# Low parts of the weights by a negative copy and an accumulating DMA, in one of two FFNs

## The chip, the cores and the metric

The kernel runs on one core of a Trainium2 chip. The metric is the time of one execution on the device in microseconds (us), median over runs. The engines are TensorE (PE, matmuls; its weight loads are listed as PEld), VectorE (DVE), ScalarE (ACT), GpSimd (POOL) and SyncE (SP, which here issues the DMAs).

## The reference

One inference step of a hybrid backbone over 128 context tokens and 512 latent tokens (640 columns), width 1024, two layers. Each layer has a token mixer (a recurrent mixer and two attentions) and then a gated FFN with a width-3 convolution on its gate half. The change concerns the FFN alone:

```python
def conv_ffn(h, lp):
    gate, val = jnp.split(h @ lp["w_up"], 2, axis=-1)
    gate = dwconv(gate, lp["ffn_conv_w"], lp["ffn_conv_b"], FFN_CONV_PAD_L)
    return (jax.nn.gelu(gate) * val) @ lp["w_down"]
...
    x = x + g2 * conv_ffn(modulate(x, lp["norm2_g"], sh2, sc2), lp)
```

Here w_up is 1024 x 5632 and w_down 2816 x 1024. All numbers are float32.

## The kernel before

Activations lie with features on the 128 partitions and tokens along the free dimension: eight chunks of 128 features by 640 columns, worked on in two halves of 320.

A float32 product is made of three matmuls in the shorter float32r type. Each operand is held as a high part (its value in float32r) and a low part (the rest, also float32r), and `mm3` (line 358) adds high x high, high x low and low x high into one bank. A weight tile of 128 x 1024 (eight blocks of 128 x 128) gives one chunk of 128 output features: per half 8 x 3 matmuls of 320 columns, so 48 matmuls for both halves (`gemm`, line 367).

`wload` (line 287) brings in such a tile. SP loads it into `wr` (line 291), ScalarE copies it into `wh`, which makes the high part (line 296), and VectorE subtracts `wh` from `wr` into `wl`, the low part (line 299). `wr`, `wh` and `wl` are rings of two buffers each (lines 206 to 208), so the weights of the chunk after next can be prepared once TensorE has finished the last chunk. In the stretch around the recurrent mixer the high part is made on VectorE instead (line 294).

The FFN (`ffn`, line 1355) starts with three gate chunks done together as the normed input comes in (`first`, line 380); the weights of two of them were brought in early by `first_weights` (line 337), those of the third by `wload` in line 1358. Then, in three groups of 8, 8 and 6 chunks, it takes turns: a gate chunk (from chunk 3 on: load in line 1373, evicted by ScalarE in lines 1334 to 1337, convolution and GELU in `ffn_gelu`, lines 1346 to 1352) and the value chunk to it (load in line 1380, multiplied onto the gate by VectorE in line 1385, and split into high and low part by lines 659 and 660). After each group `staggered` (line 1257) multiplies the group's 8 (or 6) chunks with the matching part of w_down: eight weight tiles, 1024 columns wide (768 in the last group), each result added to the residual by VectorE (line 1252). In the last group the sixth tile is split on VectorE by `wload_keys` (line 304).

The order of TensorE's work is set by `drive` (line 239), by a planned time. The other engines run their instructions in an order that a scheduler makes from dependences and priorities; `soon` (line 264) raises a priority, and line 292 raises that of the splitting a little. In each engine's queue an instruction that waits holds up all behind it. GpSimd has little to do in the FFN: three memsets of one column for each gate chunk (line 1330), which wait until the place of the pool is free.

Of the kernel before, what the change touches and what calls it, by code (L numbers as in the profile page):

```python
# [10 lines left out]
F32 = mybir.dt.float32  # L11
# [3 lines left out]
ALU = mybir.AluOpType  # L15
# [21 lines left out]
# columns of the per-feature vectors of one layer  # L37
# [6 lines left out]
# broadcast rows of one layer  # L44
# [8 lines left out]
class Slots:  # L53
    """Equal places of one tile, handed out in the order in which they came free; a place that
    another stream of work has used counts as `STRANGE` us younger."""
# [34 lines left out]
    def any_pair(self):  # L90
        """Two places wherever they are, as one operand of 2 x 512 columns."""
        a, b = sorted(self.get().at + self.get().at)
        return Slot(self.tile[:, a : b + 1 : b - a][:, :, :512], (a, b))
# [24 lines left out]
class Wide:  # L118
    """1024 columns over two places."""
# [21 lines left out]
class Stream:  # L141
    """Work whose next step may be issued `lag` us of TensorE's time after the last one, or
    once a mark has been set (and `lag` us after that)."""
# [28 lines left out]
class Net:  # L172
    NF = 22
    h_on_dve = False
    L_POOL, L_H = False, True
# [63 lines left out]
    def drive(self, streams):  # L239
        """TensorE takes its work in the order given here: the first stream that is ready."""  # L240
# [16 lines left out]
    def spawn(self, gen):  # L257
        """A stream that goes before all but the ones spawned earlier."""
        n = sum(s.spawned for s in self.streams)
        self.streams.insert(n, Stream("main", gen))  # L260
        self.streams[n].spawned = True
        self.streams[n].ready = self.t

    def soon(self, offset=None):
        """What frees a bank goes before other work of its engine."""
# [21 lines left out]
    def wload(self, src, place=None):  # L287
# [4 lines left out]
        with self.soon(self.WSOON) if self.WSOON else nullcontext():  # L292
# [4 lines left out]
            c = n // self.cut  # L297
            for o in range(0, n, c):
                self.sub_engine().tensor_tensor(  # L299
                    out=wl[:, o : o + c], in0=raw[:, o : o + c], in1=wh[:, o : o + c].bitcast(F32), op=ALU.subtract  # L300
# [3 lines left out]
    def wload_keys(self, src, low):  # L304
        """The same, the high parts behind the first weights in the place of the keys, the low ones in two of a pool."""
# [12 lines left out]
    def wload_wide(self, src, whole=False):  # L318
        """The same, into places of the two pools."""
# [17 lines left out]
    def first_weights(self, src, whole=False):  # L337
        """Weights that are there when h comes: the first in the place of the keys."""
# [19 lines left out]
    def mm3(self, out, a, b, first, last):  # L358
        """(ah + al) (bh + bl), without the product of the two low parts, which float32 can't hold"""
# [7 lines left out]
    def gemm(self, w, wofs, xs, lo, hi):  # L367
        """One output chunk over the columns lo..hi of the operands xs, into a bank."""
# [11 lines left out]
    def first(self, l, w, ws, evac):  # L380
        """The first products with h: one chunk of h after the other, as they come."""
# [15 lines left out]
    def setup(self):  # L397
# [9 lines left out]
        # silu(c) = 0.5 c (1 + tanh(c / 2))  # L407
# [9 lines left out]
    def setup_lru(self):  # L417
        nc = self.nc
        for l in range(DEPTH):
            # half biases of the recurrent gates  # L420
# [8 lines left out]
            # kk = -4 softplus(-lam); softplus(x) = max(x, 0) + log1p(e), e = exp(-|x|),  # L429
            # log1p(e) = 2 atanh(e / (2 + e))  # L430
# [20 lines left out]
    def mods(self, ahead=2):  # L451
        """The second norm's shift and scale (both conditions) of layer 0."""
# [30 lines left out]
        # chunk 4 j + b, condition i, sits in column b*128 + 32j + i  # L483
# [13 lines left out]
    def keep_cond(self):  # L497
        """silu(c) as rows, to be read by all partitions."""
# [17 lines left out]
    def mods_rows(self, l, v, pace, ahead=2):  # L516
        """One of the six modulation vectors of layer l: rows of w_mod times silu(c), summed along the row."""
# [36 lines left out]
    def square(self, x, m, half, eng=None):  # L554
        """Adds the squares of chunk m to the sums; the last chunk's stay apart."""
# [12 lines left out]
    def rstd(self, half, then=None):  # L568
        """1 / rms of every token of a half, in all partitions."""
# [28 lines left out]
        if half == 1:  # L598
            self.F.put(self.sqa, *self.sqb_)
            if then is not None:  # L600
                # the next table
# [3 lines left out]
    def modulated(self, l, w, k, half, t):  # L605
        """Chunk k of h = x * rstd * g (1 + scale) + shift, split in two parts, one half of the columns."""
# [17 lines left out]
    def norm_stream(self, l, w, half, name):  # L624
        """The norm of a half whose last chunk has just come."""
# [13 lines left out]
        else:  # L639
# [3 lines left out]
            while k < KC:  # L643
                # two chunks in one transfer where their places are in order
# [20 lines left out]
    def qkv(self, l, mx, hs):  # L665
# [8 lines left out]
        for g in range(3):  # L674
# [9 lines left out]
            for b in range(NB):  # L684
                bank = banks[b]
                if g < 2:
# [12 lines left out]
                    if b > 0:  # L699
                        # rotary of the latent q  # L700
# [25 lines left out]
        if mx == 0:  # L726
# [4 lines left out]
            # q: 1 / (8 rms), the score's scale within; k: 1 / rms  # L731
# [12 lines left out]
        # rotary of the latent k  # L744
# [13 lines left out]
    def keys(self, l, mx):  # L758
        """Both halves of every key side by side, transposed."""
# [36 lines left out]
    def attention(self, l, mx):  # L796
# [25 lines left out]
        def prepare(u):  # L822
            """What a unit needs before its scores: its q, split (turned later)."""
# [57 lines left out]
        def soften(x, lo, hi):  # L881
            """exp(score - max) of heads lo..hi, divided by its sum, from the banks."""
# [46 lines left out]
        def turn(x, lo, hi, ps):  # L929
            """The keys of a unit's probabilities into the partitions."""  # L930
# [81 lines left out]
    def lru(self, l, hs):  # L1012
        nc, io = self.nc, self.io
        self.oa, self.pend = [], deque()
        for n in range(KC):
# [34 lines left out]
            for half in range(2):  # L1050
                # 2 gelu(y) = y (1 + tanh(c0 (y + c1 y^3)))
# [25 lines left out]
    def lru_gates(self, l, oa, wg, n, xc, xch, xcl, gy):  # L1077
# [20 lines left out]
        for d in range(2):  # L1098
            # the input gate times x, twice over
# [3 lines left out]
        for d in range(2):  # L1103
            kk, nk = (self.kk[:, a, l, d * 8 + n : d * 8 + n + 1] for a in range(2))
            # log a = kk (1 + tanh); a; 1 - a^2 = tanh(-log a) (1 + a^2)
# [35 lines left out]
    def gate(self, l, row, hs, t):  # L1141
        """t = tanh(h Wg / 2) = 2 sigmoid(h Wg) - 1"""
# [577 lines left out]
```

## Time and profile before

| what | us |
|---|---|
| runs of the kernel before | 2416.93 and 2413.31, median 2415.12 |
| span of the profiled execution | 2408.8 |
| TensorE busy, of the span | 2377.8 |
| second layer's FFN with its entry and the final norm | from 1925 to 2409 of the span |

The page gives the profiled execution's time as its span, from the first to the last instruction; the time of a run holds start and end around it besides, and the median of the runs stands 6.3 us above the span. "Busy" is the time in which an engine had an instruction in work; matmuls are pipelined, so a busy TensorE need not be one at its peak. A wait is put down to the engine whose signal came last.

### The profile page before, as it was taken

The page shows a single profiled execution, that of the slowest core. Times are in us where ns is not written, and L with a number is a line of the kernel's source. Part 1 is how long each engine was busy: PE and PEld are TensorE (multiplying, and loading weights), DVE is VectorE, ACT ScalarE, POOL GpSimd, SP SyncE. Part 2 cuts the span into 40 slices and gives each one's busy share as a digit, 9 for nine tenths or more (in the row PEclk, how much of TensorE's full clock was granted, in tenths as well). Part 3 has the DMA queues.
Part 4 walks back from the last instruction along what each step waited for, and adds up shares of the span by engine and source line. Part 5 has one row for each costly group of instructions (what it writes and reads, how often), then busy time and mean ns, then how long its engine had stood idle before and what let it go on. Part 6 is the DMA issues. An engine that isn't in the chain of part 4 may idle for free.

```text
span 2408.8 us, 41835 instructions
## 1 busy us (share of the span) xinstructions
PE 2377.8 (99%) x16847; PEld 2301.7 (96%) x16847; DVE 1596.7 (66%) x3054; ACT 1006.4 (42%) x1958; POOL 17.9 (1%) x190
## 2 busy tenths in 40 slices
PE   8999999999999999999999999999999999999998
PEld 7899999998999999999999999999889999999998
DVE  6588878766766667686756688777568564344345
ACT  4237565733334322313343566565233343133232
POOL 0000000000000000000000000000000000000000
PEclk8999999999999999999999999999999999999999
DMA  8752222222452444354423222222227212222222
GB/s 284 237 191 73 83 79 76 88 75 79 146 183 75 138 140 151 130 167 148 147 87 131 89 92 70 83 85 87 69 68 230 80 62 71 79 76 73 79 68 76
DMA packets 124961, 267.73 MB, mean 111 GB/s; under 512 B 12240, under 2 KB 45536, under 8 KB 124768
## 3 DMA queue, kind: packets, MB, share of 16 engines
q1 hardware_dynamic: 124768, 265.07, 33.2%
q8 instruction: 132, 2.16, 0.4%
q14 instruction: 61, 0.50, 0.1%
HBM read 236.95 MB, written 28.07 MB: 110 GB/s over the span
## 4 chain that ended last, share of the span: by engine, by line
PE 86%; DVE 6%; ACT 3%; DMA 3%; issue 2%; SPq 0%; DVEq 0%; ACTq 0%
PE g L273 72%; PE s L273 4%; PE tb L273 4%; PE pv L273 3%; PE tb L277 3%; DVE wl L299 1%; DMA f<-in_wmodt 1%; DVE s L534 1%; ACT f L1091 1%; PE pv L277 1%; DMA f<-in_wmod 0%; DMA wr<-in_woc 0%; DVE f L1252 0%; ACT f L913 0%; DVE r L616 0%
## 5 line engine op out<-in xcount | busy, mean ns | idle before, releaser
L273 PE MATMUL g<-r,wh 128*128 128x320 f32 (+1 forms) x7920 | 1768.5, 312 | 2.9 <-ACT f L1148 0.9
L273 PEld LDWEIGHTS g<-r,wh 128*128 128x128 f32 x7920 | 1316.6, 188 | 20.5 <-issue 13.1
L273 PE MATMUL g<-r,wl 128*128 128x320 f32 (+1 forms) x3960 | 1222.3, 309 | 2.7 <-DVE wl L299 2.7
L273 PEld LDWEIGHTS g<-r,wl 128*128 128x128 f32 x3960 | 745.1, 188 | 3.8 <-DVE wl L299 3.8
L299 DVE TENSOR_TENSOR wl<-wr,wh 128x1024 fp32r<-128x1024 f32 (+2 forms) x291 | 334.8, 1151 | 224.5 <-ACT wh L296 219.6
L296 ACT CAST wh<-wr 128x1024 fp32r<-128x1024 f32 (+2 forms) x201 | 194.2, 966 | 494.9 <-PE g L273 424.4
L1252 DVE SCALAR_TENSOR_TENSOR f<-g,mod,f 128x128 f32<-128x128 f32 (+3 forms) x192 | 78.3, 435 | 138.7 <-PE g L273 138.6
L534 DVE SCALAR_TENSOR_TENSOR s<-f 128x1024 f32<-128x1024 f32 x128 | 157.2, 1228 | 15.8 <-DMA f<-in_wmodt 11.3
L891 DVE TENSOR_REDUCE sm<-s 128x1 f32<-128x640 f32 (+3 forms) x104 | 92.8, 892 | 89.1 <-PE s L273 88.6
L273 PE MATMUL g<-r 128*128 128x322 f32 (+3 forms) x632 | 124.2, 315 | 1.4 <-ACT f L1166 1.0
L273 PE MATMUL g<-wh,r 128*128 128x256 f32 x576 | 107.7, 282 | 0.0
L273 PEld LDWEIGHTS g<-r 128*128 128x128 f32 x632 | 100.4, 190 | 5.6 <-ACT f L1091 2.1
L1385 DVE TENSOR_TENSOR f<-f,g 128x320 f32<-128x320 f32 x88 | 42.5, 486 | 91.7 <-PE g L273 56.1
L659 ACT CAST r<-f 128x640 fp32r<-128x640 f32 (+2 forms) x98 | 70.3, 720 | 65.7 <-PE s L273 27.0
L273 PEld LDWEIGHTS g<-wh,r 128*128 128x128 f32 x576 | 90.4, 188 | 3.4 <-issue 3.4
L273 PE MATMUL s<-k,r 128*128 128x320 f32 (+3 forms) x448 | 92.3, 326 | 0.9 <-ACT k L787 0.9
L660 DVE TENSOR_TENSOR r<-f,r 128x640 fp32r<-128x640 f32 (+2 forms) x98 | 79.1, 812 | 15.8 <-ACT r L659 8.4
L913 ACT ACTIVATE f<-s,sm,rs 128x640 f32<-128x640 f32 (+1 forms) x80 | 63.5, 796 | 62.0 <-DVE sm L895 44.9
L1348 DVE SCALAR_TENSOR_TENSOR f<-f,vec 128x641 f32<-128x641 f32 x88 | 77.8, 887 | 13.6 <-ACT f L1346 8.4
L913 ACT ACTIVATE f<-s,sm 128x384 f32<-128x384 f32 (+2 forms) x80 | 45.6, 577 | 92.8 <-DVE sm L900 71.0
L273 PE MATMUL g<-wl,r 128*128 128x256 f32 x288 | 81.1, 282 | 0.0
L277 PE MATMUL tb<-ident,f 128*128 128x128 f32 x576 | 79.7, 272 | 0.0
(202 smaller groups left out, 2472.6 us busy)
## 6 DMA issues: line engine op xcount, KB each, us to landing
wr<-in_wup SPq DMA_DIRECT2D x84, 512.0 KB, 3.2
wr<-in_win SPq DMA_DIRECT2D x77, 512.0 KB, 3.3
f<-in_wmodt SPq DMA_DIRECT2D x64, 512.0 KB, 4.1
f<-in_wmod SPq DMA_DIRECT2D x64, 256.0 KB, 4.6
wr<-in_wdown SPq DMA_DIRECT2D x32, 512.0 KB, 3.4
wr<-in_wqkv SPq DMA_DIRECT2D x24, 512.0 KB, 3.6
g_kept<-f SPq DMA_DIRECT2D x32, 320.0 KB, 2.3
f<-g_kept SPq DMA_DIRECT2D x32, 320.0 KB, 3.7
```

The source lines that it names most:

```text
L273: self.nc.tensor.matmul(**kw)
L277: self.nc.tensor.transpose(out, in_, self.ident)
L296: nc.scalar.copy(wh[:, :n], raw[:, :n])
L299: self.sub_engine().tensor_tensor(out=wl[:, o : o + c], in0=raw[:, o : o + c], in1=wh[:, o : o + c].bitcast(F32), op=ALU.subtract)
L534: nc.vector.scalar_tensor_tensor(out=self.S, in0=w.ap, scalar=1.0, in1=self.cb[i].ap, op0=ALU.mult, op1=ALU.mult, accum_out=self.mod[:, l, ...
L659: nc.scalar.copy(xh[:, :n], t[:, :n])
L660: (eng or nc.vector).tensor_tensor(out=xl[:, :n], in0=t[:, :n], in1=xh[:, :n].bitcast(F32), op=ALU.subtract)
L891: nc.vector.tensor_reduce(out=m_[:, lo:hi], in_=src, axis=AX.XY if hi - lo == 1 else AX.X, op=ALU.max)
L913: nc.scalar.activation(out=p[:, :n].rearrange("p (a c) -> p a c", a=2) if hi - lo == 1 else p[:, o : o + n], in_=src if hi - lo == 1 else ...
L1252: self.nc.vector.scalar_tensor_tensor(out=dst[:, lo:hi], in0=b[:, lo - c0 : hi - c0], scalar=self.mod[:, l, gate + m, i : i + 1], in1=src[ ...
L1348: nc.vector.scalar_tensor_tensor(out=g[:, :n], in0=gp[:, k : k + n], scalar=fw(k), in1=g[:, :n], op0=ALU.mult, op1=ALU.add)
L1385: nc.vector.tensor_tensor(out=gp[:, lo:hi], in0=gp[:, lo:hi], in1=b, op=ALU.mult)
```

## The change

In the FFN of the second layer (`l == 1`) `wload` makes the low part in another way. ScalarE writes the negative of the raw weights into `wl`, which is rounded to float32r as the high part is; GpSimd then issues a DMA that adds the raw weights onto it, so that raw minus rounded is left. VectorE has no part in it. The switch is set at the start of `ffn`, so the weights loaded in line 1358 and all after it go this way: 42 tiles of w_up and 23 of w_down, 65 in all. The two early tiles of w_up and the tile of `wload_keys` stay on VectorE.

```diff
 class Net:
+    by_dma = False
...
     def wload(self, src, place=None):
...
-            c = n // self.cut
-            for o in range(0, n, c):
+            if self.by_dma:
+                nc.scalar.mul(wl[:, :n], raw[:, :n], -1.0)
+                nc.gpsimd.dma_start(out=wl[:, :n], in_=raw[:, :n], accum_op=ALU.add)
+            else:
                 self.sub_engine().tensor_tensor(
-                    out=wl[:, o : o + c], in0=raw[:, o : o + c], in1=wh[:, o : o + c].bitcast(F32), op=ALU.subtract
+                    out=wl[:, :n], in0=raw[:, :n], in1=wh[:, :n].bitcast(F32), op=ALU.subtract
                 )
...
     def ffn(self, l):
         nc, io = self.nc, self.io
+        self.by_dma = l == 1
```

The loop over pieces of a tile, which is taken out as well, made one piece everywhere (`cut` is 1). The rest of the diff is comments and doc strings. The changed kernel's lines are some three to four numbers higher.

The order of the engines' queues ahead of the second FFN is the same in both kernels. In it, ScalarE's queue is shown for one gate and one value chunk in the second group of eight. `wh_65` and `wl_67` are the buffers of the gate's weights, `wh_66` and `wl_68` those of the value's, `g` the banks. Before:

```order
L1334 COPY f<-g_74 128x128 [waits PE_49]
L1335 COPY f<-g_74 128x192
L296 CAST wh_65<-wr_63 128x1024 [waits DMAHW4_49,PE_49]
L1337 COPY f<-g_72 128x320 [waits PE_49]
L1346 ACTIVATE f<-f,vec 128x641 [waits Activation_49,Pool_49]
L1351 ACTIVATE f<-f 128x128 [waits DVE_49,Activation_49]
L1352 ACTIVATE f<-f 128x512
L296 CAST wh_66<-wr_64 128x1024 [waits DMAHW5_49,PE_49]
L659 CAST r<-f 128x640 [waits DVE_49,Activation_49]
```

Now:

```order
L1337 COPY f<-g_74 128x128 [waits PE_49]
L1338 COPY f<-g_74 128x192
L297 CAST wh_65<-wr_63 128x1024 [waits DMAHW4_49,PE_49]
L1340 COPY f<-g_72 128x320 [waits PE_49]
L299 ACTIVATE wl_67<-wr_63 128x1024 [waits DMASW0_49]
L1349 ACTIVATE f<-f,vec 128x641 [waits Activation_49,Pool_49]
L1354 ACTIVATE f<-f 128x128 [waits DVE_49,Activation_49]
L1355 ACTIVATE f<-f 128x512
L297 CAST wh_66<-wr_64 128x1024 [waits DMAHW5_49,PE_49]
L299 ACTIVATE wl_68<-wr_64 128x1024 [waits DMASW1_49,PE_49]
L662 CAST r<-f 128x640 [waits DVE_49,Activation_49]
```

The negative copies (L299) have come in: the gate's behind the eviction of the gate's second half, the value's right behind its cast and ahead of the split of the finished chunk.

GpSimd's queue in the first group, where the memsets of line 1330 (1333 now) prepare the next gate chunk. Before:

```order
L1330 MEMSET f 128x1 [waits DMAHW5_49,DMAHW2_49,DMAHW7_49,PE_49,Activation_49]
L1330 MEMSET f 128x1 [waits PE_49,Activation_49]
L1330 MEMSET f 128x1 [waits DMAHW2_49,Activation_49]
L1330 MEMSET f 128x1 [waits Activation_49]
L1330 MEMSET f 128x1 [waits DVE_49]
L1330 MEMSET f 128x1 [waits DMAHW7_49,DMAHW4_49,Activation_49]
```

Now, over one pair of chunks:

```order
L1333 MEMSET f 128x1 [waits Activation_49] x2
L300 DMA wl_68<-wr_64 128x1024 [waits DMAHW1_49,Activation_49]
L300 DMA wl_67<-wr_63 128x1024 [waits DMASW0_49,DMAHW2_49,PE_49,Activation_49]
L1333 MEMSET f 128x1 [waits DVE_49]
L1333 MEMSET f 128x1 [waits Activation_49,Pool_49] x2
L300 DMA wl_68<-wr_64 128x1024 [waits DMAHW3_49,DMASW1_49,Activation_49]
```

The accumulating DMAs (L300) stand between the memsets, the value's and the next gate's one behind the other. SP's queue keeps its order; its raw loads in this FFN wait for the accumulating DMA (and ScalarE) where they waited for VectorE.

## Rows read from the trace of the kernel before

**Rows 1.** The page's busy times: engine, us (share of span), instructions.

```profile
span 2408.8 us, 41835 instructions
...
PE 2377.8 (99%) x16847; PEld 2301.7 (96%) x16847; DVE 1596.7 (66%) x3054; ACT 1006.4 (42%) x1958; POOL 17.9 (1%) x190
```

**Rows 2.** Busy us of each engine in stretches of the second layer's FFN.

```profile
core 0: us, PE busy (x) PEld busy (x) DVE busy (x) ACT busy (x) POOL busy (x), PEclk, DMA share, GB/s
1925.00:1945.00 20.00, 19.61 (x136) 19.12 (x136) 18.47 (x50) 12.31 (x32) 0.20 (x2) 1.00 0.16 54
1945.00:2352.00 407.00, 407.00 (x2784) 406.96 (x2783) 167.64 (x220) 130.00 (x208) 5.31 (x54) 1.00 0.22 73
...
2395.00:2409.00 14.00, 4.66 (x37) 4.23 (x36) 9.32 (x23) 1.00 (x3) 0.00 (x0) 0.74 0.54 187
```

**Rows 3.** What PE waited for, 1925 to 2409 us: total, times, longest.

```profile
PE g L273 <- DVE f L1252: 0.4, 1, 0.4
PE g L273 <- DVE r L660: 0.2, 1, 0.2
```

**Rows 4.** ScalarE in order of time: start us, us, instruction [idle before <- releaser].

```profile
2114.42 1.05 ACT L296 CAST wh<-wr 128x1024 fp32r<-128x1024 f32 x1 [1.85 <-PE g L273]
2115.38 0.72 ACT L659 CAST r<-f 128x640 fp32r<-128x640 f32 x1
...
2121.44 1.05 ACT L296 CAST wh<-wr 128x1024 fp32r<-128x1024 f32 x1 [2.87 <-PE g L273]
2122.39 0.42 ACT L1337 COPY f<-g 128x320 f32<-128x320 f32 x1
2122.91 0.93 ACT L1346 ACTIVATE f<-f,vec 128x641 f32<-128x641 f32 x1
...
2128.46 1.05 ACT L296 CAST wh<-wr 128x1024 fp32r<-128x1024 f32 x1 [1.85 <-PE g L273]
```

**Rows 5.** Groups of instructions, 1941 to 2409 us: count | busy, mean ns | idle.

```profile
L299 DVE TENSOR_TENSOR wl<-wr,wh 128x1024 fp32r<-128x1024 f32 x56 | 68.6, 1225 | 107.7 <-ACT wh L296 107.7
L296 ACT CAST wh<-wr 128x1024 fp32r<-128x1024 f32 x56 | 58.8, 1050 | 189.4 <-PE g L273 181.1 <-issue 8.3
```

**Rows 6.** DMA issues of the whole span: count, KB each, median us to landing.

```profile
wr<-in_wup SPq DMA_DIRECT2D x84, 512.0 KB, 3.2
wr<-in_win SPq DMA_DIRECT2D x77, 512.0 KB, 3.3
...
wr<-in_wdown SPq DMA_DIRECT2D x14, 384.0 KB, 3.0
f<-in_x SPq DMA_DIRECT2D x16, 320.0 KB, 4.9
...
wr<-in_wob SPq DMA_DIRECT2D x16, 256.0 KB, 2.6
```

**Rows 7.** ScalarE in the last down-projection, in order of time.

```profile
2358.94 0.83 ACT L296 CAST wh<-wr 128x768 fp32r<-128x768 f32 x1 [0.71 <-PE g L273]
2359.68 0.41 ACT L561 ACTIVATE f<-f 128x256 f32<-128x256 f32 x1
...
2364.25 0.83 ACT L296 CAST wh<-wr 128x768 fp32r<-128x768 f32 x1 [0.75 <-PE g L273]
```

**Rows 8.** ScalarE at the entry of the FFN, in order of time.

```profile
1925.59 1.03 ACT L296 CAST wh<-wr 128x1024 fp32r<-128x1024 f32 x1
1926.52 0.47 ACT L564 ACTIVATE f<-f 128x320 f32<-128x320 f32 x1
```

**Rows 9.** PE at the entry of the FFN, in order of time.

```profile
1930.57 0.32 PE L273 MATMUL g<-r,wl 128*128 128x320 f32 x1
```

**Rows 10.** ScalarE behind the first products, in order of time.

```profile
1954.09 1.06 ACT L296 CAST wh<-wr 128x1024 fp32r<-128x1024 f32 x1
1955.04 0.93 ACT L1346 ACTIVATE f<-f,vec 128x641 f32<-128x641 f32 x1
...
1959.88 1.05 ACT L296 CAST wh<-wr 128x1024 fp32r<-128x1024 f32 x1 [0.23 <-PE g L273]
```

## The prediction

> **What bounds the kernel now.** The order of reading is: the page's busy times, the same by stretches, what TensorE waits for in the stretch that the change touches, the groups of instructions there, one period of that stretch in order of time, and last the transfers.
>
> The busy times say that TensorE (PE) works in 99% of the 2408.8 us and VectorE (DVE) in 66% [rows 1]. A share over the whole span hides the stages, so the stretches come next. In the second layer's FFN, from 1945 to 2352 us, PE is busy in 407.00 of 407.00 us at a granted clock of 1.00, the 2.4 GHz level, while VectorE has 167.64 us of work and ScalarE (ACT) 130.00 [rows 2]. So in this stretch an instruction taken from VectorE buys nothing by itself: VectorE idles for 239 us of it already. The list of PE's waits from the entry of the FFN to the end confirms it: apart from two waits of the final norm, PE waits 0.4 us at the entry and 0.2 us at the last group [rows 3]. The most that this change can win is about these 0.6 us.
>
> What matters is therefore how late a low part (wl) may come before PE has to wait for it. One set of weights feeds 48 matmuls. Two sets of buffers take turns, so a buffer that PE leaves must be filled again while PE works on the other set. A cast of the high part (line 296) starts when PE leaves a buffer; three of them in a row start at 2114.42, 2121.44 and 2128.46 [rows 4]: PE needs 7.02 us for a set, 0.146 us for a matmul. The first two matmuls of a set use the high part, so the low part is wanted 0.29 us after the set begins. From the start of the cast to that moment there are 7.02 + 0.29 = 7.31 us. Before, the cast (1.05 us) and VectorE's subtraction (1.23 us) [rows 5] filled about 2.3 of them, and 5 us were left over. That is the cover of this edit, and the question is whether it is thick enough.
>
> **What is removed.** 65 subtractions leave VectorE; 56 of them take 68.6 us in the FFN [rows 5]. By the paragraph above they hide beside PE, so I count them at nothing. Two stand in the entry, where VectorE has 18.47 us of work in 20 [rows 2] and PE's whole wait is 0.4 us [rows 3]; at most that goes, and I count nothing for it either.
>
> **What is added.** For each of the 65 weight sets ScalarE makes a negative copy, and GpSimd issues an accumulating DMA of 512 KB (384 KB for seven of them) from the raw weights onto it. No negative copy stands in the trace. The nearest row is the cast of the same shape, 1.05 us [rows 5]; it reads and writes the same bytes on the same engine, so the copy is taken as 1.05 us, between 0.95 (the distance at which the next instruction starts behind a cast, [rows 4]) and twice as much. ScalarE has room for 65 of these: 130 us of work in 407.
>
> Where it stands decides more. In the down-projections and for the value weights the copy follows its cast directly: the next instruction starts 0.96 us behind the cast (2115.38 against 2114.42) and the copy ends 0.96 + 1.05 = 2.01 us after the buffer came free. For the gate weights the eviction of a bank (line 1337, 0.42 us) stands between them, and the instruction behind that starts at 2122.91, 1.47 us after the cast; the copy ends at 2.52 us [rows 4]. So the DMA, from the end of the copy to the first matmul that reads its result, has 7.31 - 2.01 = 5.30 us in a down-projection and 7.31 - 2.52 = 4.79 us for a gate. Call the DMA's whole time L: the wait on GpSimd, the making of descriptors, the transfer and the signal. What L is above this room, PE waits.
>
> **How long is L?** Nothing in the trace accumulates, and GpSimd issues no transfer, so I bound it by the loads that SP issues [rows 6]. Issue to landing is 2.6 us for 256 KB, 3.0 for 384 and 3.2 to 3.3 for 512. The lower end is one plain pass of 512 KB, 3.3 us: it fits into both rooms. If the DMA only reads two streams instead of one, 256 KB more cost 0.7 us, so a second 512 KB cost 1.4 and L = 4.7; this fits as well, by a hair for the gates. If the sum waits for the destination to be read back, as two transfers one after the other, L = 2 x 3.3 = 6.6. The upper end is two passes at the slowest landing of the trace, 4.9 us (f<-in_x, at the kernel's busy start), so L = 9.8. I take 6.6: the destination must be read and written, the 16 DMA engines also carry the raw weights (a mean share of 0.22 here, [rows 2]), and GpSimd has to make the descriptors, for which the row of the plain load has no term.
>
> The Trainium skill speaks against this change, but not with one voice. "DMA: Bandwidth & Descriptors", Anatomy of one DMA, fits GpSimd's transfers by 2.0 us plus bytes over 436 GB/s: 3.2 us for a plain 512 KB, which the landings of SP's loads here agree with. "Collectives: The Full Stack", The bandwidth ceiling, says that an add in the DMA costs because it reads two sources; two reads by that fit give an estimate of 4.4 us, and the sum below would shrink to the first rival. The same DMA page, Bandwidth, has 6.15 us of engine time for 1 MB from GpSimd, before descriptors; by that estimate L lies above both rooms. No run here shows either.
>
> **The sum, at L = 6.6.**
> - Gate and value chunks: a pair of sets cannot turn faster than the gate's buffer: 2.52 + 6.6 + (7.02 - 0.29) = 15.85 us against 14.04, so each pair loses 6.6 - 4.79 = 1.81. There are 19 pairs (chunks 3 to 21): 34.4 us.
> - The two full down-projections, 16 sets: two sets lose 6.6 - 5.30 = 1.30, so 8 x 1.30 = 10.4.
> - Last down-projection, 768 columns: casts 5.31 us apart (2358.94, 2364.25), cast and copy 0.74 + 0.83, so the room is 5.31 + 0.3 - 1.57 = 4.0 us [rows 7]; the DMA has 384 KB, 2 x 3.0 = 6.0 [rows 6]. Two sets lose 2.0; its first two sets and the one on VectorE have more room, so two such pairs: 4.0.
> - Entry: the cast of the third up chunk starts at 1925.59, the next instruction at 1926.52 [rows 8], so its copy ends at 1927.57 and its low part lands at 1934.2. PE wanted it at 1930.57 [rows 9]: 3.6.
> - Behind the first products: cast at 1954.09, next at 1955.04 [rows 10], copy to 1956.09, landing 1962.7. PE leaves the set before it at 1959.88 and wants the low part at 1960.17: 2.5. One more turn of the same buffer, 1.3.
>
> Together 56 us. PE's clock is taken as kept: it is granted 1.00 where PE is busy 19.61 of 20 us and 0.74 where it is busy 4.66 of 14 [rows 2]; at 14.04 of 15.85 it stands near the first. Two queues could add to it and don't: the raw load on SP now waits for the DMA instead of the subtraction, but it needs 3.3 us and is wanted a set later; GpSimd's memsets stand behind the DMA, but each waits for the same gate chunk's GELU anyway. The profiled execution becomes 2408.8 + 56 = 2465 us; the median of the runs stands 6.3 us above that span (start and end around it), so 2415.1 + 56 = 2471 us, 2.3% slower. Each us of L is worth 32 us (19 + 8 + 5 single places), and 2%, about what a measurement of this kernel can tell from no change, is 48 us: the verdict turns at L = 6.35.
>
> **The rivals.**
> - *The transfer hides* (not slower). The add runs in the stream and L is at most about 5.5; at 4.7 only the entry (1927.57 + 4.7 - 1930.57 = 1.7 us) and the first value sets (0.6) lose, and the last group's split, which now stands behind a copy of 0.84 us on ScalarE, adds its delay to the 0.2 us of wait there: about 3 us, 2418. For it: the landing grows so little with size, and DMA engines are idle for 78% of the stretch. Against it: the room for the gates is 4.79 us, and GpSimd's own work comes off it. It decides below L = 5.5 (up to 21 us).
> - *The add is slow.* Read back, add and write come to 9.8 us: 56 + 3.2 x 32 = 158, 2573. For it: three times as many bytes pass the engines as for a load, in the same rows as the raw loads. Against it: nothing in the trace is that slow at 512 KB.
> - *VectorE was a bound after all.* Its 68.6 us would show as waits of PE on it; there are 0.6 us of these [rows 3]. At best 2414.5.
>
> **How the numbers follow.** Forecast, two passes with L between 5.5 and 8.5: 0.50, of which 0.12 lies below 6.35 and so within 2%; its own range is 2436 to 2532. The transfer hides: 0.33. The add is slow, beyond 8.5: 0.15. VectorE a bound: 0.02. Slower is 0.38 + 0.15 = 0.53, same 0.33 + 0.12 = 0.45, faster 0.02. The range goes from the hidden transfer, 2416, to 2575, the upper end of L.
>
> **What would show it.** Right: in the FFN of the second layer PE waits for the DMA of wl once in two sets; casts of line 296 follow each other about 7.9 us apart instead of 7.02; landing behind the copy is near 6.6 us; VectorE's work falls by some 70 us with no wait of PE gone. The step on the copy is wrong if it takes over 1.2 us; the step on the room if PE waits on ScalarE. The whole is wrong if landings stay under 4.8 us, or if PE's clock falls in the waits.

## The result, and the profile after

The changed kernel takes 2442.68 us (median of 2 runs, 2439.80 to 2445.56), against 2415.12 us before: a ratio of 1.0116, 95% interval 1.0082 to 1.0150. It is slower by 27.6 us, about half of the forecast 56 us; that is clear of no change, but less than 2%. The time lies in the range, which is wide: 2416 to 2575 goes from no change to 6.6% slower. It is neither the forecast (2471) nor the first rival (2418), but between them, and the reason for this is what the experiments are about.

Busy times of the page of the changed kernel, which answer to [rows 1], and the new queue of GpSimd (packets, MB, share of 16 engines' span):

```profile
span 2437.8 us, 41968 instructions
...
PE 2389.4 (98%) x16847; PEld 2309.3 (95%) x16847; DVE 1522.6 (62%) x2989; ACT 1064.8 (44%) x2023; POOL 74.0 (3%) x255
...
q0 software_dynamic: 9360, 33.17, 7.0%
```

VectorE lost 74 us of work and ScalarE gained 58, as the edit says. TensorE has the same 16847 matmuls, and yet 11.6 us more busy time. The span is 29.0 us longer, so TensorE's idle time grew by 17.4 us. That is two losses, and only one of them is waiting. They are found next in the stretches (engine busy us, count, then PE's granted clock, DMA share and GB/s):

```profile
1925.00:1935.00 10.00, 7.86 (x45) 7.37 (x44) 5.87 (x18) 4.77 (x11) 1.52 (x2) 0.83 0.75 156
1945.00:2090.00 145.00, 143.25 (x974) 142.20 (x973) 36.76 (x61) 63.06 (x91) 18.30 (x39) 1.00 0.56 135
2094.00:2104.00 10.00, 7.10 (x29) 7.10 (x30) 0.92 (x3) 0.00 (x0) 0.00 (x0) 0.66 0.39 96
2110.00:2120.00 10.00, 7.16 (x39) 6.90 (x38) 0.55 (x1) 2.49 (x4) 0.86 (x1) 0.83 0.83 183
2120.00:2270.00 150.00, 148.78 (x1015) 148.15 (x1014) 35.44 (x57) 66.25 (x96) 20.41 (x45) 1.00 0.60 146
2275.00:2285.00 10.00, 7.15 (x30) 7.15 (x31) 1.48 (x5) 0.00 (x0) 0.00 (x0) 0.66 0.39 98
2291.00:2301.00 10.00, 7.17 (x39) 6.90 (x38) 0.55 (x1) 2.49 (x4) 0.86 (x1) 0.83 0.84 186
2301.00:2380.00 79.00, 78.72 (x538) 78.37 (x537) 20.15 (x28) 39.44 (x62) 10.44 (x21) 1.00 0.57 139
```

Against [rows 2], where PE was busy in all of the stretch at a clock of 1.00, the long stretches (145, 150 and 79 us) lose 1.75, 1.22 and 0.28 us. Most of the loss sits in four places of about 10 us, two and two, and some of it at the entry (1925 to 1935). In each of the four PE stands for nearly 3 us, and the granted clock around it is below 1. What PE waited for, 1925 us to the end (total, times, longest), against [rows 3]:

```profile
PE g L274 <- DMA wl<-wr: 17.8, 12, 3.1
...
PE g L274 <- ACT f L1338: 0.5, 1, 0.5
PE g L274 <- ACT r L618: 0.5, 1, 0.5
```

Single rows of PE in order of time (start us, us, instruction, idle before and its releaser): the first products at the entry, the one behind them, and two of the four long waits, the first with its neighbours.

```profile
1927.04 0.53 PE L274 MATMUL g<-r,wh 128*128 128x320 f32 x2 [0.48 <-ACT r L618]
1929.23 0.63 PE L274 MATMUL g<-r,wl 128*128 128x320 f32 x1 [1.66 <-DMA wl<-wr]
...
1961.56 0.42 PE L274 MATMUL g<-r,wl 128*128 128x320 f32 x1 [0.56 <-DMA wl<-wr]
...
2096.90 0.63 PE L274 MATMUL g<-r,wl 128*128 128x320 f32 x1 [3.09 <-DMA wl<-wr]
...
2097.86 0.47 PE L274 MATMUL g<-r,wl 128*128 128x320 f32 x1
2098.13 0.73 PE L274 MATMUL g<-r,wh 128*128 128x320 f32 x2
...
2103.71 0.31 PE L274 MATMUL g<-r,wl 128*128 128x320 f32 x1
2103.86 0.46 PE L274 MATMUL g<-r,wh 128*128 128x320 f32 x2
...
2113.31 0.64 PE L274 MATMUL g<-r,wl 128*128 128x320 f32 x1 [2.84 <-DMA wl<-wr]
```

The other two long waits are of 2.89 us (to 2277.85) and 2.83 us (to 2294.24). Behind the first of them a matmul takes 0.27 us (2097.86 to 2098.13), at 2103.71 it takes 0.15 us again: the two levels of the clock, 1.2 and 2.4 GHz. A granted clock of 0.66 in 10 us is 6.8 us at the half level, 0.83 is 3.4 us; over the four places and the entry that makes 24 us, which cost about 12 us of matmul time. That is the growth of the busy time.

ScalarE and GpSimd in the steady part and at the first long wait (ScalarE's rows answer to [rows 4]):

```profile
2089.93 1.05 ACT L297 CAST wh<-wr 128x1024 fp32r<-128x1024 f32 x1 [5.02 <-PE g L274]
2090.89 1.05 ACT L299 ACTIVATE wl<-wr 128x1024 fp32r<-128x1024 f32 x1
...
2135.76 1.05 ACT L297 CAST wh<-wr 128x1024 fp32r<-128x1024 f32 x1 [2.88 <-PE g L274]
2136.71 0.42 ACT L1340 COPY f<-g 128x320 f32<-128x320 f32 x1
2137.03 1.06 ACT L299 ACTIVATE wl<-wr 128x1024 fp32r<-128x1024 f32 x1
...
2142.78 1.05 ACT L297 CAST wh<-wr 128x1024 fp32r<-128x1024 f32 x1 [1.11 <-PE g L274]
```

```profile
2092.23 0.86 POOL L300 DMA_DIRECT2D wl<-wr  x1 [6.17 <-ACT wl L299]
```

The steady casts still follow each other 7.02 us apart: the pairs of gate and value chunks lose almost nothing (three single waits in 19 pairs, of 0.80, 1.13 and 0.28 us). The groups and the DMA issues from 1941 and 1930 us on, against [rows 5, 6] (the DMA's last number is from the start of GpSimd's instruction to landing):

```profile
L299 ACT ACTIVATE wl<-wr 128x1024 fp32r<-128x1024 f32 x56 | 59.2, 1057 | 0.0
L300 POOL DMA_DIRECT2D wl<-wr x63 | 54.2, 860 | 354.7 <-ACT wl L299 344.9 <-ACT f L564 6.0 <-ACT f L567 3.8
```

```profile
wl<-wr POOLq DMA_DIRECT2D x56, 512.0 KB, 4.4
...
wl<-wr POOLq DMA_DIRECT2D x7, 384.0 KB, 3.8
```

The copy ends at 2091.94 us, GpSimd starts at 2092.23, 0.29 us later, and the landing takes 4.4 us: L, as the prediction defined it, is 4.7 us and not 6.6.

**Where the four long waits come from.** They stand at the eighth tile of each of the two full down-projections, and at the first gate tile behind it. The last two tiles of a down-projection are taken half by half (`staggered`, late = 2): first half of tile seven, first half of tile eight, second half of seven, second half of eight. So PE leaves tile six's buffer, works half a set (24 matmuls, 3.51 us), and wants tile eight in that same buffer. At the other end it leaves tile seven's buffer, has half a set of tile eight to do, and wants the next gate. The room is 3.51 + 0.29 = 3.80 us there, not 7.31. The path is cast and copy 2.01, GpSimd's start 0.29, landing 4.4: 6.7 us. The difference is 2.9 us, four times.

### The profile page after: what moved, and what is told of

Its sections match the earlier page's. It is cut to its first block, busy times and chain, and to the rows that moved or that the text cites. A ratio compares the mean times of both kernels' runs of the same rounds, so it can differ in the third digit from the quotient of the medians.

```text
span 2437.8 us, 41968 instructions
## 1 busy us (share of the span) xinstructions
PE 2389.4 (98%) x16847; PEld 2309.3 (95%) x16847; DVE 1522.6 (62%) x2989; ACT 1064.8 (44%) x2023; POOL 74.0 (3%) x255
## 3 DMA queue, kind: packets, MB, share of 16 engines
q0 software_dynamic: 9360, 33.17, 7.0%
## 4 chain that ended last, share of the span: by engine, by line
PE 79%; DVE 7%; DMA 5%; issue 4%; ACT 4%; SPq 0%; POOL 0%; DVEq 0%; ACTq 0%; POOLq 0%
PE g L274 65%; PE s L274 4%; PE tb L274 3%; PE pv L274 3%; PE tb L278 3%; DMA wl<-wr 2%; DMA f<-in_wmodt 2%; DVE s L537 1%; DVE wl L302 1%; ACT f L1094 1%; PE pv L278 1%; DMA wr<-in_woc 0%; ACT wh L297 0%; DMA f<-in_wmod 0%; ACT f L916 0%
## 5 line engine op out<-in xcount | busy, mean ns | idle before, releaser
L274 PE MATMUL g<-r,wl 128*128 128x320 f32 (+1 forms) x3960 | 1228.3, 310 | 21.9 <-DMA wl<-wr 17.8
L302 DVE TENSOR_TENSOR wl<-wr,wh 128x1024 fp32r<-128x1024 f32 (+2 forms) x226 | 257.4, 1139 | 109.2 <-ACT wh L297 97.9
L537 DVE SCALAR_TENSOR_TENSOR s<-f 128x1024 f32<-128x1024 f32 x128 | 157.4, 1230 | 16.8 <-DMA f<-in_wmodt 11.7
```

Source lines behind the costliest of these rows:

```text
L274: self.nc.tensor.matmul(**kw)
L302: self.sub_engine().tensor_tensor(out=wl[:, :n], in0=raw[:, :n], in1=wh[:, :n].bitcast(F32), op=ALU.subtract)
L537: nc.vector.scalar_tensor_tensor(out=self.S, in0=w.ap, scalar=1.0, in1=self.cb[i].ap, op0=ALU.mult, op1=ALU.mult, accum_out=self.mod[:, l, ...
```

## The experiments

My theory after this: (a) the loss of the stream is these four places, where the room is half a set; (b) each costs its wait and then the half clock behind it; (c) L is 4.7 us because the addition reads a second source. The rivals: the rest of the DMA traffic costs TensorE something everywhere; ScalarE's added copies do; the clock falls because of the DMA traffic and not because PE stood; the addition is free and GpSimd's transfers are that slow anyway.

Single spans scatter by some us before the FFN begins. So the table has, beside the medians, the stage's time in the profiled execution: from the start of PE's first wait at the FFN's entry to the start of its last waiting matmul in the final norm. For before and after these are the rows (a wait starts at the row's start less the idle time in brackets):

```profile
1930.20 0.54 PE L273 MATMUL g<-r,wh 128*128 128x320 f32 x2 [0.38 <-DVE f L1252]
...
2401.22 0.82 PE L273 MATMUL pv<-v,ones 128*128 128x128 f32 x4 [1.26 <-DVE v L588]
```

```profile
2430.13 0.68 PE L274 MATMUL pv<-v,ones 128*128 128x128 f32 x4 [1.26 <-DVE v L591]
```

Before: 2401.22 - 1929.82 = 471.4 us. After: 2430.13 - 1926.56 = 503.6. Runs e1 to e12 were taken in four rounds, each with the kernel before beside it (2410.8 to 2412.9 us), so it is the ratios that compare from row to row.

| run | edit | median us | ratio, 95% interval | stage, against before | PE's waits on wl |
|---|---|---|---|---|---|
| after | the change | 2442.7 | 1.0116, 1.0082 to 1.0150 | +32.2 | 17.8 in 12 |
| e1 | four short tiles back on VectorE | 2423.3 | 1.0045, 1.0029 to 1.0061 | +9.4 | 5.8 in 8 |
| e2 | these four alone by DMA | 2429.0 | 1.0071, 1.0058 to 1.0084 | +18.3 | 11.5 in 4 |
| e3 | third low buffer | 2421.8 | 1.0039, 1.0025 to 1.0053 | +11.1 | 1.7 in 1, and 3.9 in 1 on the third buffer |
| e4 | copies without DMA | 2415.3 | 1.0013, 1.0003 to 1.0024 | +2.3 | none |
| e5 | no half-by-half tiles | 2423.4 | 1.0045, 1.0030 to 1.0059 | +11.1 | 5.2 in 8 |
| e6 | the same order in the kernel before | 2412.3 | 1.0008, 0.9998 to 1.0017 | 0.0 | none |
| e7 | waits made on VectorE | 2438.8 | 1.0113, 1.0095 to 1.0131 | +27.0 | 18.0 in 4 (VectorE) |
| e8 | DMA without the addition | 2419.4 | 1.0033, 1.0022 to 1.0043 | +7.8 | 5.3 in 4 |
| e9 | copy written ahead of the cast | 2439.3 | 1.0113, 1.0098 to 1.0128 | +25.6 | 16.0 in 11 |
| e10 | shorter waits on VectorE | 2419.5 | 1.0031, 1.0020 to 1.0042 | +5.8 | 4.7 in 4 (VectorE) |
| e11 | e9 and e3 together | 2419.1 | 1.0034, 1.0021 to 1.0048 | +8.0 | 0.7 in 1, and 3.9 in 1 on the third buffer |
| e12 | cast on VectorE | 2426.8 | 1.0062, 1.0047 to 1.0077 | +17.4 | 10.4 in 8 |

**e1 and e2: the four short tiles, taken out and alone.** `short` is true for the last tile of the two full down-projections and for the first gate tile of the next group; the diff is e1's, e2 has `and short` in the second line.

```
-            if self.by_dma:
+            if self.by_dma and not short:
...
-        ws += [self.wload(src(m)) for m in ms[len(ws):]]
+        ws += [self.wload(src(m), short=after is None and m == KC - 1) for m in ms[len(ws):]]
...
-                    w = self.wload(io["wup"][l, j])
+                    w = self.wload(io["wup"][l, j], short=j == c0 and c0 > 0)
```

> Four of the 65 tiles go back to VectorE: the eighth tile of each of the two full down-projections and the gate tile that follows each. The changed kernel's trace has PE waits of 3.09, 2.84, 2.89 and 2.83 us on just these and a granted clock of 0.50 for some 20 us behind them. Theory (short tiles: PE works only half a set, 3.5 us, between leaving the buffer and wanting it again, and its clock falls behind the wait): 11.6 us of waits and some 10 us of slow clock go, 2421 us, and no fall of the clock is left between the entry and the end. Rival (the loss is spread over all 65 DMAs by their traffic): 4 of 65 parts of 28 us go, 2441 us. Rival (ScalarE's copies cost): 2441 us as well.

> The counterpart: only these four tiles take the negative copy and the accumulating DMA, the other 61 stay on VectorE. Theory (short tiles and clock): waits of about 2.9 us at the four places and the falls of the clock stay, 2415 + 22 = 2437 us. Rival (spread over all DMAs, or over ScalarE's copies): 4 of 65 parts, 2417 us.

In e1 the four waits are gone, no wait behind the entry is over 1.3 us, and the clock keeps its full level from the entry to the end of the stream:

```profile
1945.00:2380.00 435.00, 430.93 (x2928) 428.21 (x2927) 114.24 (x189) 188.88 (x282) 53.45 (x110) 1.00 0.55 137
```

PE's four rows in e2 that waited for wl:

```profile
2092.73 0.42 PE L274 MATMUL g<-r,wl 128*128 128x320 f32 x1 [2.94 <-DMA wl<-wr]
2107.97 0.63 PE L274 MATMUL g<-r,wl 128*128 128x320 f32 x1 [2.85 <-DMA wl<-wr]
2270.47 0.42 PE L274 MATMUL g<-r,wl 128*128 128x320 f32 x1 [2.84 <-DMA wl<-wr]
2285.65 0.64 PE L274 MATMUL g<-r,wl 128*128 128x320 f32 x1 [2.82 <-DMA wl<-wr]
```

Four DMAs of 65 bring 17 of the 28 us by the ratios (0.71 of 1.16%), and the other 61 bring 0.45%: together 1.16%, the whole. e2's stage closes almost exactly: 11.5 us of waits and 13.6 us at half clock, which cost 6.8, are 18.3. Its time came 8 us under the expectation; the half clock was shorter than at the same places of the changed kernel (13.6 against 20.4 us), which is 3.4 of them, and the kernel before ran 2.2 us lower in this round (2412.9) than the 2415 that the expectation starts from.

**e3: a third low buffer** behind the first products, in the place of the keys.

```
+        if l == 1:
+            self.wl.tiles.append(self.K2.rearrange("p a b -> p (a b)")[:, :D])
```

> All 65 tiles by DMA, but behind the first products the low parts have three buffers in turn (the third lies where the first weights were), so that the negative copy and the DMA can run one set earlier. Theory (the room is too short at a few places): each low part has 3.5 us or more besides, all waits but the entry's go, 2415 to 2420 us. Rival (the DMA's traffic or ScalarE's copies cost): the same work is done, 2435 to 2443 us.

All waits in the stream are gone, the four among them:

```profile
1970.00:2380.00 410.00, 410.00 (x2803) 410.00 (x2802) 97.61 (x163) 179.79 (x259) 55.76 (x108) 1.00 0.61 149
```

That settles the rival of the traffic: with the DMA engines busy at a share of 0.61, TensorE works without a gap and takes 0.146 us for a matmul (410.00 / 2803), as before [rows 2]. What is left is the entry, and one wait that the edit itself makes: 3.87 us to 1962.47 us, where the third buffer (under the name k) is filled for the first time. Half clock goes with both, 3.4 us at the entry and 6.8 at the filling; 1.7 and 3.9 us of waits and half of 10.2 make 10.7 of the stage's 11.1. The time came a little over the expected 2415 to 2420.

**e4: the copies without the DMAs.** VectorE's subtraction writes over them.

```
-                nc.gpsimd.dma_start(out=wl[:, :n], in_=raw[:, :n], accum_op=ALU.add)
-            else:
...
+            self.sub_engine().tensor_tensor(
```

> ScalarE makes the 65 negative copies, but no DMA adds to them: VectorE's subtraction overwrites them as before. Theory: 65 copies of 1.06 us hide in ScalarE's idle time, but the subtraction comes 1 us later; at the short tiles the room is 3.8 us and cast, copy and subtraction need 3.3, so no wait: 2415 to 2418 us. Rival (ScalarE's copies cost, by the delay of its other work): 2425 us or more.

ScalarE's 65 copies cost about 3 us (0.13%, interval 0.03 to 0.24%). Twice, at a group's end, the last split stands behind a copy and PE waits 0.72 us.

**e5 and e6: no tiles half by half**, in the changed kernel and, as a control, in the kernel before.

```
-        late = self.LATE if after is not None else 2
+        late = self.LATE if after is not None else (0 if l == 1 else 2)
```

> The changed kernel, but the two full down-projections of the second layer take all eight tiles one after the other, none half by half, so each buffer of the low parts has a whole set (7.0 us of TensorE) between its release and its next use. My theory (the lost time sits where only half a set lies between, and in the clock that falls after those waits) expects the four waits of 2.8 to 3.1 us gone, no fall of the clock between 1945 and 2380 us, and about the time of the run with the four short tiles on VectorE: 2418 to 2424 us. The rival (the four waits belong to the boundary itself: the weights of the next group come late there, or ScalarE is busy with the gates) expects them at the same places and 2437 us or more.

> The kernel before with the same change of order and nothing else: the two full down-projections of the second layer take their tiles one after the other. It shows what the order alone is worth: by my theory nothing, 2410 to 2416 us, since TensorE waits nowhere there before. The rival, that the order of the halves hides work of VectorE at the group's end (residual sums ahead of the next gates), expects new waits of about 1 us each and 2417 us or more.

PE's busy time in a long stretch of e5:

```profile
1945.00:2380.00 435.00, 430.77 (x2921) 427.48 (x2920) 109.28 (x183) 192.33 (x286) 56.92 (x114) 1.00 0.58 141
```

The four waits are gone and the clock is 1.00 from 1945 to 2380 us, as in e1 and with nearly e1's time, though every weight set still goes by DMA. The control shows that the order by itself costs nothing that can be told from zero (1.0008, 0.9998 to 1.0017). So the waits do not belong to the boundary between the groups, but to the half set.

**e7 and e10: the same places, late for another reason.** No new DMA; VectorE repeats its subtraction four times (e7) or twice (e10).

```
-            for o in range(0, n, c):
+            for o in [0] * (1 + again):
...
+        ws += [self.wload(src(m), again=4 * (l == 1 and after is None and m == KC - 1)) for m in ms[len(ws):]]
```

> The kernel before, without any of the new DMAs; at the four places of the long waits VectorE makes the same subtraction five times over (four more, 1.2 us each), so that the low parts come late there for another reason. The room at these places is 3.8 us, of which cast and first subtraction take 2.3, so waits of 2 to 3.5 us. By my theory a wait of that size costs itself and the clock behind it, whoever caused it: the granted clock falls to half behind these waits as well, and the time is 2424 to 2433 us. The rival (the clock falls because of the traffic of the accumulating DMAs) expects the waits without the fall: no half clock in the stream, and 2420 to 2426 us.

> The kernel before, without the new DMAs; at the four places VectorE makes its subtraction three times over (two more). In the run with four more the waits were 3.9 to 5.3 us, two subtractions of 1.2 us less leave 1.5 to 2.9. It asks from what wait on the clock falls: by my theory waits under about 1.7 us leave it (those of 1.3 in the run without the accumulation did), and longer ones may not, so 2417 to 2428 us. The rival, that any wait there brings the fall, expects half clock behind each of the four and 2426 us or more.

e7: the first of its four waits, and the stretches that hold each.

```profile
2092.71 0.63 PE L273 MATMUL g<-r,wl 128*128 128x320 f32 x1 [3.94 <-DVE wl L299]
```

```profile
2092.00:2102.00 10.00, 9.29 (x45) 9.29 (x46) 1.33 (x3) 0.00 (x0) 0.00 (x0) 0.67 0.16 52
2110.00:2120.00 10.00, 8.99 (x47) 8.99 (x48) 0.95 (x1) 0.49 (x2) 0.00 (x0) 0.72 0.34 107
2275.00:2285.00 10.00, 9.66 (x55) 9.67 (x56) 2.07 (x6) 1.05 (x1) 0.00 (x0) 0.83 0.15 52
2292.00:2302.00 10.00, 8.99 (x50) 8.99 (x51) 0.95 (x1) 0.93 (x3) 0.00 (x0) 0.77 0.26 93
```

The clock falls behind all four, without any accumulating DMA and with a DMA share of 0.15 to 0.34. So it is the standing engine that brings the fall, and the traffic is not needed for it; e1, e3 and e5 have the traffic (shares of 0.55 to 0.61) and no fall in the stream. The waits became longer than expected (3.9 to 5.3 us, because other work of VectorE came between the repeats), and so did the time. In e10 the waits were 0.98, 0.95, 0.97 and 1.78 us, shorter than the expected 1.5 to 2.9, and the clock stayed at 1.00 from 1945 to 2380 us; the time is 1.0031 of before.

**e8: the DMA without the addition.**

```
-                nc.gpsimd.dma_start(out=wl[:, :n], in_=raw[:, :n], accum_op=ALU.add)
+                nc.gpsimd.dma_start(out=wl[:, :n], in_=raw[:, :n])
```

> The changed kernel with the same GpSimd DMAs of the same sizes but without the accumulation (the addition is left out: the low buffer then holds the raw weights). If the addition, that is a second source to be read, is what makes a row of 4 KB take 0.33 us, rows take about 0.2 us as those of the raw loads do, the landing of 512 KB falls from 4.4 to about 3.3 us, the four long waits shrink to about 1.8 us each and the time to 2426 to 2434 us. The rival (the addition is free and the time is that of any GpSimd DMA of this size) expects the landing at 4.4 us, the same four waits of 2.8 to 3.1 us and 2438 to 2444 us.

GpSimd's group from 1941 us on, and its queue and issues on the page of e8:

```profile
L300 POOL DMA_DIRECT2D wl<-wr x63 | 33.3, 528 | 347.6 <-ACT wl L299 331.3 <-ACT f L567 9.5 <-DMA wr<-in_wup 6.8
```

```profile
q0 software_dynamic: 9360, 33.17, 3.7%
...
wl<-wr POOLq DMA_DIRECT2D x58, 512.0 KB, 2.9
```

The same bytes in the same 9360 packets take 3.7% of the engines' span, against 7.0% with the addition; the landing falls from 4.4 to 2.9 us, of which 0.33 us is GpSimd's shorter instruction (528 against 860 ns). The four waits fall to 1.3 us, the clock stays, and the time falls by 0.83% (20 us). The direction is as expected, the size larger: I had expected 3.3 us and 2426 us or more. The addition costs 1.5 us for each 512 KB: 0.33 us of GpSimd's instruction and 1.2 us of the engines' time, which is nearly that of a second pass (1.4 us for a transfer here, 2.6 with the addition).

**e9, e11 and e12: 1 us less on the way.** e9 writes the negative copy and the DMA ahead of the cast in `wload`; e11 adds e3's third buffer to it. e12 moves the cast to VectorE:

```
-            if self.h_on_dve and self.L_H:
+            if self.by_dma or self.h_on_dve and self.L_H:
```

> The changed kernel with the negative copy ahead of the cast on ScalarE, so that each of the new DMAs starts about 1 us earlier. By my theory (the four long waits are the path of 6.7 us from release to landing, less the room of 3.8) each of the four shrinks from 2.8 to 3.1 us to about 1.9; if the clock still falls behind them 2432 to 2440 us, if it doesn't 2424 to 2430. The rival (the cast comes late now and the high parts are waited for in its place) expects waits of TensorE on ScalarE's cast in every set and 2440 us or more.

> Both together: the changed kernel with the negative copy ahead of the cast and the third buffer of low parts behind the first products. With the DMAs 1 us earlier and a whole set of room more, my theory expects no wait on a low part between 1970 and 2380 us and at most the entry's waits of 2 to 4 us, so 2414 to 2420 us: level with the kernel before, not faster, since TensorE is busy all the time there. The rival (the traffic itself costs TensorE something beside the waits) expects 2421 us or more, as in the run with three buffers alone.

> The changed kernel with the cast of the high parts moved to VectorE in the second layer's FFN, so that the negative copy is the first thing that ScalarE does after the release. (The run that wrote the copy ahead of the cast in the code left the scheduler's order at the four places as it was, so that it told nothing on this.) From release to landing are then 0.1 + 1.06 + 0.29 + 4.4 = 5.8 us instead of 6.7, less the room of 3.8: by my theory each of the four long waits shrinks to 1.8 to 2.2 us. If the clock still falls behind them, as it did behind 2.8 and not behind 1.8, 2430 to 2438 us; if it doesn't, 2419 to 2428. The rival (landing is later when it starts earlier, because it then meets other transfers) expects the waits at 2.8 us and 2436 us or more.

e9 missed, and told nothing on its question: ScalarE's rows at the first place show that the scheduler left the cast ahead.

```profile
2095.57 1.05 ACT L300 CAST wh<-wr 128x1024 fp32r<-128x1024 f32 x1 [5.02 <-PE g L274]
2096.53 1.05 ACT L295 ACTIVATE wl<-wr 128x1024 fp32r<-128x1024 f32 x1
```

Its four waits are 2.88, 3.12, 2.89 and 2.84 us, as in the changed kernel; it is in effect that kernel measured again, but for the entry, where the copy did come first and the wait fell from 1.66 to 0.69 us. In e12 the copy really comes first, and the four waits are these:

```profile
2092.68 0.41 PE L274 MATMUL g<-r,wl 128*128 128x320 f32 x1 [2.08 <-DMA wl<-wr]
...
2107.05 0.41 PE L274 MATMUL g<-r,wl 128*128 128x320 f32 x1 [2.02 <-DMA wl<-wr]
...
2269.36 0.41 PE L274 MATMUL g<-r,wl 128*128 128x320 f32 x1 [2.05 <-DMA wl<-wr]
2282.15 0.41 PE L274 MATMUL g<-r,wl 128*128 128x320 f32 x1 [1.99 <-DMA wl<-wr]
```

5.8 less 3.8 is 2.0: path less room, to a tenth. The clock fell behind two of the four (0.83 in the 10 us around each of the first two, 1.00 around the others), and the time, 2426.8, is at the upper end of the better case. e11 has no wait on a low part in the stream and is 0.34% slower than before, by the entry's 0.7 us, the 3.9 us of the third buffer's first filling and 6.8 us at half clock with it (3.4 lost): 8.0 together, as the stage says. No version beats the kernel before, and none could by much: there PE waits 0.6 us from the entry to the last group [rows 3].

## Why the prediction was right and wrong

**What bounds the kernel: right.** 74 us taken from VectorE took no wait of PE away.

**The copy: right.** 1.057 us against 1.05, and in a down-projection its end comes 2.01 us after the cast's start, as worked out.

**L = 6.6 us: wrong, and the step behind the size of the forecast.** It was "two transfers one after the other"; measured are 0.29 + 4.4 = 4.7 us, the value that the prediction had for two streams read in one pass. That is under the 4.8 us below which the prediction called the whole of it wrong; nor did PE wait once in two sets (12 waits on wl in 65 tiles), nor did the casts move to 7.9 us apart. e8 shows that it is the addition that makes the difference to a plain transfer: 1.5 us. The estimate of 4.4 us from the Trainium skill ("Collectives: The Full Stack", The bandwidth ceiling, with the fit in "DMA: Bandwidth & Descriptors", Anatomy of one DMA) is the landing of 4.4 us that the trace shows; the plain transfer's 3.2 us by the same fit stands against 2.9 in e8. The Trainium skill's figure of 6.15 us of engine time for 1 MB from HBM ("DMA: Bandwidth & Descriptors", Bandwidth) is not what these rows within SBUF show: 7.0% of 2437.8 us over 65 transfers is 2.6 us for one with the addition, and 3.7% of 2416.2 us is 1.4 without.

**Pairs, 34.4 us: 2.2 us.** With L = 4.7 below the room of 4.79 they fit, and the casts stay 7.02 us apart; only three single landings came late.

**The two down-projections, 10.4 us: 11.7 us, for another reason.** The step "8 x (L - 5.30)" took every tile to have a whole set of room; by it, L = 4.7 gives nothing. The trace has no wait on wl over 0.2 us there but 3.09, 2.84, 2.89 and 2.83 us at the eighth tiles and the gate tiles behind them, where the room is 3.80 us. The prediction had not looked at the half-by-half order of the last two tiles, neither for the forecast nor for the first rival. e1, e2, e3 and e5 each show it from another side, e12 the arithmetic. That the two sums are alike is chance.

**"PE's clock is taken as kept": wrong**, and named as what would make the whole wrong. About 12 us at the four places and the entry. It was read from stretches of 14 and 20 us; the falls come behind waits of 2 to 3 us in a stream that is otherwise full. e7, which has falls without the traffic, and e1, e3 and e5, which have the traffic and no fall in the stream, show that they follow the wait.

**The single places: right by the rival's L.** At 4.7 the prediction had 1.7 us for the entry and 0.6 for the first value sets; the trace has 1.66 and 0.56. In the last down-projection the room of 4.0 us stands against 0.29 + 3.8 = 4.1; it lost 0.67 and 0.81 us in two waits, for which 0.1 each would have been due. Ahead of the first GpSimd started 0.97 us after the copy instead of 0.29; the DMA ahead of the second landed after 5.5 us instead of 3.8.

**"Each us of L is worth 32 us": wrong.** From e8 to the changed kernel L grows by 1.5 us and the time by 20 us, so 13 us for each. The pairs and most of the down-projection have slack below L = 4.8; four places do not, and they pay in clock as well.

**The 2%: the verdict came out the other way.** The prediction gave "slower" by 2% or more 0.53 and "same" 0.45, and took 2% for about what a measurement can tell. The runs can tell far smaller differences: their intervals reach some 0.1 to 0.3% to either side.

So sign and range held by luck more than by the mechanism, and both signs that the prediction had named for "the whole is wrong" came. L was 1.9 us too large, which put 53 us too much into the sum (56 less the 3 of the first rival). What it did not have put much of the measured time back: in the trace the waits at the four short tiles (11.7 us) and the half clock (12 us with the entry's).

Single landings come late elsewhere too (waits of 0.2 to 1.1 us in the changed kernel, at other places in each run). No run was made on this, but the trace of the changed kernel has a hint. The DMAs ahead of the waits of 0.80, 0.20 and 1.13 us landed after 5.6, 5.2 and 6.2 us instead of 4.4, and that of the 0.81 us in the last down-projection after 5.5 instead of 3.8. While each was under way, one packet of the page's queue "instruction" (16 KB) ran as well. For the 1.13 us, from 2173 to 2179.4 us:

```profile
q8 instruction: 1, 0.02, 1.7%
...
wl<-wr POOLq DMA_DIRECT2D x1, 512.0 KB, 6.2
```

Other DMAs met such a packet and were less than 0.5 us late, so this is a coincidence in time and not a shown cause.

## What to carry to other kernels

Before a slower path fills a buffer, look for the shortest time between the release of that buffer and its next use, not the usual one: an order that splits tiles in halves cuts the room to a half in a few places, and here four of 65 transfers made 60% of the loss. A wait of some 3 us in a full stream of matmuls is to be priced at up to twice its length, because the clock behind it may be halved for a while. An accumulating DMA is to be priced at about twice the engine time of a plain one (1.9 times here).

## What the runs showed of the hardware

- An accumulating DMA of 512 KB from GpSimd within the chip's SBUF landed 4.4 us after its start (384 KB: 3.8), the plain one after 2.9 (2.6). GpSimd's own instruction took 860 against 528 ns, and the engines' time for the same packets was 1.9 times as much (7.0 against 3.7% of the span). This fits the second source read that the Trainium skill names as the cost of an add ("Collectives: The Full Stack", The bandwidth ceiling), and is seen here within one core; the runs show the factor, not its reason.
- TensorE's clock fell to 1.2 GHz behind single waits in an otherwise full stream. Behind the eight waits of 0.9 to 1.8 us at the four places of e8 and e10 it never did; behind those of 2.0 us in e12 in two of four; behind those of 2.8 us and more in four of four, in each of the changed kernel, e2 and e7, and in three of four in e9. It isn't the wait alone: at the entry the same 1.66 us brought a fall in the changed kernel, e3 and e5 and none in e1.
- DMA traffic by itself took nothing from TensorE: with the DMA engines at a share of 0.61 it worked 410.00 of 410.00 us at full clock (e3, 1970 to 2380 us).
